# Prompt attention of a streaming encoder: score rows shared between six PSUM banks, and softmax steps and sample copies issued at raised priority

## The chip, the cores and the metric

The kernel runs on one core of one Trainium2 chip. The metric is device time in microseconds (us) of the whole program: three runs of the kernel before gave 2592.65, 2591.31 and 2591.14, the median is 2591.31. Less is better.

A core has several engines, each with a queue of its own: TensorE (PE in the profile; PEld is its weight load) multiplies matrices and transposes, VectorE (DVE) and ScalarE (ACT) do elementwise work, GpSimd (POOL) does some copies and issues some transfers, SyncE (SP) issues most transfers. An engine takes the instructions of its queue in order; a semaphore holds an instruction until its operands are there or its buffer is free. TensorE writes into PSUM, eight banks of 128 partitions by 2 KB; the other engines read them from there.

## The reference

Two groups of frames go through the same two layers with the same weights: a prompt of 512 frames (one stream), and 8 samples of 16 frames each, that continue running streams with 256 cached keys. Cut to what matters:

```python
for l in range(DEPTH):                                   # 2 layers, width 1024
    x = x + 0.5 * swiglu(rmsnorm(x, norm_ffn1[l]), w_ffn1_gu[l], w_ffn1_down[l])   # inner width 2816
    h = rmsnorm(x, norm_mix[l])
    cb, cc, cv, q, k, v, g = split(h @ w_in[l])          # 3 x 512 | 3 x 512 | 2 x 1024
    y_conv = cb * causal_depthwise_conv3(cc * cv)
    s = (q @ k.T) * 64 ** -0.5 + rel_bias                # 8 heads x 64; masked to -1e30:
    y_attn = softmax(where(valid, s, -1e30)) @ v         # own chunk of 64 and the 8 before
    m = sigmoid(g_c) * (y_conv @ w_conv_out) + sigmoid(g_a) * (y_attn @ w_attn_out)
    x = x + m @ w_o
    x = x + 0.5 * swiglu(rmsnorm(x, norm_ffn2[l]), w_ffn2_gu[l], w_ffn2_down[l])
y = rmsnorm(x, norm_final)
```

All data are f32. In the prompt, each frame sees every frame of its own chunk of 64 and all before it (there are only 512), so the scores are a block triangle: row block i (128 queries) has (i + 1) x 128 keys.

## The kernel before

**Staging.** All 640 frames (512 prompt, 128 sample) lie transposed in SBUF, 640 columns wide. Per layer come a feed-forward block, the mixer (projection, convolution, attention, merge) and a second feed-forward block. Weights come from HBM once, in slabs of 128 x 1024 (`load`, L199). To reach f32 accuracy, a slab is split into a rounded part `whi` (ScalarE's cast, L264) and the remainder `wlo` (VectorE, L269), and a product takes three matmuls: whi by xhi, whi by xlo, wlo by xhi. Three slabs of each are kept. `flush` issues remainders that are still pending, `slab` the next slabs' preparation.

**Products in sevens.** A 2 x 2 block product is done in seven block products instead of eight, in the manner of Strassen, over the halves of 320 frames. In the mixer `seven` (L664) does that: products into the PSUM tiles `ma` (the first, third, fifth and last), `mb` (the second) and `mc` (the fourth and sixth). Between them ScalarE and VectorE take intermediate sums out (`c1`, `u2`, `c5`, and the functions `first`, `second`, `third`, `last`). One half of a block product is one step; `seven` is a generator that yields after each, 14 in all. `both` (L908) calls it for q and k, and for the convolution's columns; `gate_pair` (the one at L922) for gates.

**Attention.** `attention` (L1104) computes v, and q and k of the first two heads. Then it goes through four pairs of heads. Its order is written out at the end of the prompt part: `fill(n)` takes n steps of the generator `stream`, which holds the products still to do (q and k of the other pairs, convolution, gates), and so puts them between the parts of the attention:

```python
        fill(2)
        scores(0)
        fill(14)
        for p in range(npair):
            if p + 1 < npair:
                scores(p + 1)
                fill(4)
            vals = values(p)
...
```

- `scores(p)` (L1181): for each of four row blocks, in the order 0, 1, 3, 2, one PSUM tile `pss` per head and one matmul per head (L1200). VectorE then adds the bias and takes the row maximum in one instruction (L1203) and writes the scores into SBUF (`ycp` tiles, named `yc`, for even pairs, `s` tiles for odd pairs). The maxima stand in row 0 of a small tile `st`.
- `weigh` (L1210) calls `softmax` (L1346): VectorE negates the maxima (L1350), ScalarE takes the exponentials and their sums (L1352), VectorE takes the reciprocals (L1354). Then ScalarE scales the four row blocks of a head by them (L1214).
- `values(p)` (L1217): eight groups of transposes of the weights on TensorE (L1227) into tiles `ptp`, copied out by VectorE for the even head and by ScalarE for the odd one, then the products with v into `py`, which ScalarE copies (L1243). Parts of `stream` lie between.
- The samples follow, one after the other: `sscores(b)`, with the same `softmax` inside a raised priority, and `svalues(b)` (L1298). After every fourth sample a bank of transposed results, `ptx`, goes to the tile `yas` (`ya`) by two copies (L1328): VectorE's for the lower 64 partitions, ScalarE's for the upper.

Behind the attention `outputs` (L1018) does the other gate pairs; in each the product tiles are named `qa`, `qb` and `qc`.

**PSUM in the mixer.** `layout("a", 0)` (L158) makes two pools of four banks: `att` for everything of the attention (`pss`, `ptp`, `py` and the samples' tiles), and `pr` for the products (`ma`, `mb`, `mc`). A tile takes the next buffer of its pool in rotation; who writes it first waits until the buffer's previous tile has been read. `seven` asks for its three tiles at its start (L667).

**What sets the order.** In the attention only TensorE's order is the program's (`manual_schedule` for PE, L949). VectorE's, ScalarE's, GpSimd's and SyncE's orders are made when the program is built, by the framework's scheduler: it goes by dependences and by a priority, which is the position in the program. `soon()` (L324) lifts what stands under it by 300 positions, `weights()` in `seven` by 150. So where an instruction stands in VectorE's queue is set by its own position and by whether others were lifted past it. In `outputs` and the feed-forward blocks all of PE, DVE and ACT go in program order.

Of the kernel before, what the change touches and what calls it, by code (L numbers as in the profile page):

```python
# [13 lines left out]
ALU = mybir.AluOpType  # L14
PSUM = bass.MemoryType.PSUM

P = 128
D = 1024
L = 2
SEQ = 512  # L20
NB = 8
TS = 16
T = SEQ + NB * TS
HT = T // 2
PAST = 256
H = 8
HD = 64
# [11 lines left out]
NEG = -1e30  # L39
# [103 lines left out]
def trunk(ctx: ExitStack, tc: tile.TileContext, xin, wst, small, pbias, samplebias, kcache, vcache,  # L143
          yout, ko, vo, co):
    nc = tc.nc
    PE, DVE, ACT, POOL, SP = nc.tensor, nc.vector, nc.scalar, nc.gpsimd, nc.sync
# [24 lines left out]
    def att(name):  # L171
        return banks["att"].tile([P, 512], F32, tag="att", name=name)
# [14 lines left out]
    slabs, n = [], 0  # L187
# [79 lines left out]
    def flush():  # L267
        for lo, src, hi in pending:
            DVE.tensor_tensor(out=lo, in0=src, in1=hi.bitcast(F32), op=ALU.subtract)  # L269
        pending.clear()  # L270
# [16 lines left out]
    def ahead():  # L287

        source(len(ready))

    def begin():

        prep(used[0] + 2)
# [6 lines left out]
    def chunk():  # L300
        return slab()[0]
# [22 lines left out]
    def soon():  # L324
        return tc.high_priority(offset=300)
# [19 lines left out]
    def block(ps, s, half, ops, ks, start, stop):  # L345

        for kp in ks:
            w = [z[:, (half * NP + kp) * P : (half * NP + kp + 1) * P] for z in s]
            xh, xl = ops(kp)
            for j, (a, b) in enumerate(((w[0], xh), (w[0], xl), (w[1], xh))):  # L350
                PE.matmul(ps, a, b, start=start and kp == 0 and j == 0,  # L351
                          stop=stop and kp == NP - 1 and j == 2, skip_group_check=True)
# [16 lines left out]
    for k in range(KT):  # L369
# [4 lines left out]
        if k % 2 == 0:  # L374
            c = slice(k * P, (k + 2) * P)
# [68 lines left out]
    class Expand(Stats):  # L444
# [72 lines left out]
        def weights(self, m):  # L517


            if m == KT - 3:  # L520
                source(used[0] + 3)
            elif m == KT - 1:
                self.flush()
                ahead()
                flush()
                begin()
# [137 lines left out]
    def seven(n, bank, X, c1, u2, c5, first, second, third, last):  # L664


        pa, pb, pc = (bank(f"m{i}{n}")[:, :HT] for i in "abc")  # L667

        def mul(ps, s, half, x, start):
            for ks in (range(NP // 2), range(NP // 2, NP)):  # L670
                block(ps, s, half, x, ks, start, True)
                yield

        def weights():
            with tc.high_priority(offset=150):
                return chunk()

        s = weights()
        yield from mul(pa, s, 0, X["11"], True)
        with soon():  # L680
            ACT.copy(c1, pa)
        yield from mul(pb, s, 1, X["21"], True)
        with soon():
            first(pb)
        s = weights()
        yield from mul(pa, s, 0, X["N6"], False)
        with soon():
            ACT.copy(u2, pa)
        yield from mul(pc, s, 1, X["T5"], True)
        with soon():  # L690
            ACT.copy(c5, pc)
        s = weights()
        yield from mul(pa, s, 0, X["T7"], False)
        with soon():
            second(pa)
        yield from mul(pc, s, 1, X["22"], False)
        with soon():
            third(pc)
        s = weights()
        yield from mul(pa, s, 0, X["T4"], False)  # L700
        with soon():
            last(pa)
# [401 lines left out]
    def attention(l, h, norms, stats, ops, mp, yas, ycp, both, others):  # L1104
# [3 lines left out]
        npair = H // 2  # L1108
        nt = T // P
        NQ = SEQ // P  # L1110
# [5 lines left out]
        qa, ka = {}, {}  # L1116
# [32 lines left out]
        for c in range(KT // 2):  # L1149
            wh, wl = chunk()  # L1150
            for kk in range(2):
# [3 lines left out]
                for t in range(nt):  # L1155
                    for j, (w, xx) in enumerate(((wh, xh), (wh, xl), (wl, xh))):
                        PE.matmul(pv[t], xx[:, t * P : (t + 1) * P],  # L1157
                                  w[:, kk * AW : (kk + 1) * AW],
                                  start=c == 0 and kk == 0 and j == 0,
                                  stop=c == KT // 2 - 1 and kk == 1 and j == 2)  # L1160
# [16 lines left out]
        offs = [sum(P * (i + 1) for i in range(n)) for n in range(NQ)]  # L1177

        weights = {}

        def scores(p):  # L1181

            heads = [2 * p + e for e in range(2)]
            bias, ss, st = [], [], []
            for hh in heads:
                n = f"{l}_{hh}"
                bias.append(mp.tile([P, SEQ], F32, name=f"bias{n}", tag="bias"))
                POOL.dma_start(bias[-1], pbias[l, hh])
                POOL.memset(bias[-1][0:CHUNK, SEQ - CHUNK :], NEG)

                ss.append(mp.tile([P, offs[-1] + SEQ], F32, name=f"s{n}", tag="s") if p % 2
                          else ycp[hh % 2].rearrange("p a t -> p (a t)"))
                st.append(mp.tile([P, 4, NQ], F32, name=f"st{n}", tag="st", bufs=4))

            for i in (0, 1, NQ - 1, *range(2, NQ - 1)):
                w = (i + 1) * P
                pss = [att(f"pss{l}_{hh}_{i}")[:, :w] for hh in heads]
                for e in range(2):
                    r = slice(e * HD, (e + 1) * HD)
                    PE.matmul(pss[e], qa[p][r, i * P : (i + 1) * P], ka[p][r, :w], start=True, stop=True)  # L1200
                for e in range(2):
                    with soon():
                        DVE.tensor_tensor_reduce(  # L1203
                            out=ss[e][:, offs[i] : offs[i] + w], in0=pss[e], in1=bias[e][:, SEQ - w :],
                            scale=1.0, scalar=NEG, op0=ALU.add, op1=ALU.max,
                            accum_out=st[e][:, 0, i : i + 1])
            for e, hh in enumerate(heads):
                weigh(hh, ss[e], st[e])

        def weigh(hh, s, st):  # L1210
            parts = [(offs[i], (i + 1) * P) for i in range(NQ)]
            softmax(s, st, parts)
            for i, (o, w) in enumerate(parts):
                ACT.activation(s[:, o : o + w], s[:, o : o + w], AF.Copy, scale=st[:, 3, i : i + 1])  # L1214
            weights[hh] = s
# [49 lines left out]
        G = 4  # L1265
        held, ptx = {}, [None]
# [31 lines left out]
        def svalues(b):  # L1298
            n = f"{l}_{b}"
            box, st, vraw, vn = held[b]  # L1300
            s = box[:, :KS]
            pt = box[:, KS : KS + 2 * P].rearrange("p (a b) -> p a b", a=2)
            pn, yx = (box[:n, KS + o * P : KS + (o + 1) * P] for n, o in ((TS, 2), (P, 3)))
            ptp = att(f"sptp{n}")
            for j in range(2):
                PE.transpose(ptp[:, j * P : (j + 1) * P], s[:, j * P : (j + 1) * P], ident)
            PE.transpose(ptp[:TS, 2 * P : 3 * P], s[:, PAST:], ident)
            with soon():
                ACT.copy(pt, ptp[:, : 2 * P].rearrange("p (a b) -> p a b", a=2))
                DVE.tensor_copy(pn, ptp[:TS, 2 * P : 3 * P])  # L1310
            yield

            pys = att(f"spy{n}")[:, :P]
            for j, (w, v) in enumerate(((pn, vn), (pt[:, 0], vraw[:, 0]), (pt[:, 1], vraw[:, 1]))):
                for p in range(npair):
                    r = slice(32 * p, 32 * p + 32)
                    PE.matmul(pys[r], w[:, r], v[:, p * P : (p + 1) * P], start=j == 0, stop=j == 2)
            with soon():
                ACT.activation(yx, pys, AF.Copy, scale=st[:, 3, 0:1])
            yield  # L1320
            if b % G == 0:
                ptx[0] = att(f"ptx{n}")
            PE.transpose(ptx[0][:, (b % G) * P : (b % G + 1) * P], yx, ident)
            if b % G == G - 1:
                c0 = SEQ + (b + 1 - G) * TS
                for e in range(2):
                    r = slice(e * HD, (e + 1) * HD)
                    (ACT.copy if e else DVE.tensor_copy)(  # L1328
                        yas[r, :, c0 : c0 + G * TS].rearrange("p a (b t) -> p a b t", b=G),
                        ptx[0][r].rearrange("p (b a e t) -> p a b e t", b=G, a=npair, e=2)[:, :, :, e, :])  # L1330

        sscores(0)
        sscores(1)
        for b in range(NB):
            vals = svalues(b)
            fill(4)
            next(vals)
            fill(3)
            if b + 2 < NB:
                sscores(b + 2)  # L1340
            next(vals)
            fill(2)
            next(vals, None)
        fill(KT * KT)

    def softmax(s, st, parts):  # L1346


        n = len(parts)
        DVE.tensor_scalar(out=st[:, 1, :n], in0=st[:, 0, :n], scalar1=-1.0, scalar2=None, op0=ALU.mult)  # L1350
        for i, (o, w) in enumerate(parts):
            ACT.activation(s[:, o : o + w], s[:, o : o + w], AF.Exp, bias=st[:, 1, i : i + 1],  # L1352
                           accum_out=st[:, 2, i : i + 1])
        DVE.reciprocal(st[:, 3, :n], st[:, 2, :n])  # L1354

    def conv(l, c, pair, upper, c5, rr2, cn, y):

# [278 lines left out]
```

## Time and profile before

The profiled execution is one run of its own, with its own time.

| what | value | where |
|---|---|---|
| median of three runs | 2591.31 us | times |
| time of the profiled execution | 2593.46 us | times |
| its span | 2591.4 us | profile, first line |
| mean granted TensorE clock | 0.997 | cores |
| TensorE at work between 492.15 and 672.53 us (layer 0), 1771.6 and 1951.09 us (layer 1) on the attention and what lies between | 180.4 and 179.5 us | timeline |

How to read it: the page begins with each engine's busy time and its share of the span, then shows the span in forty slices, the transfers, the chain of work that ended last (followed back from the last instruction), and the costliest groups of instructions. A group is named by its line in the code, its engine, its operation and its tiles (`out<-in`, buffer numbers left out). The trace behind the page is asked for other views: waits (which instruction waited, what released it, total, times and longest in us), a timeline (start, duration, engine, line, operation, and in brackets the idle time before it with its releaser), and windows (each engine's busy time in a stretch, with the granted TensorE clock). Duration and idle time of a matmul are modelled: TensorE starts the next before the last has drained, so that a matmul of 320 columns is listed with 0.31 us and the next starts some 0.147 us later.

### The profile page before, as it was taken

What the parts mean: (1) busy time and instruction counts of PE and PEld (TensorE: products, weight loads), DVE (VectorE), ACT (ScalarE), POOL (GpSimd) and SP (SyncE); (2) the same over time, 40 slices, a digit from 0 to 9 for tenths busy, and PEclk for the clock granted to TensorE, in tenths of its full rate; (3) what the DMA queues carried; (4) which work ended last, traced back from release to release, by engine and by line L of the source; (5) the groups of instructions that cost most, each with busy time, mean ns of one, the idle gap of its engine ahead of it and who ended that gap; (6) DMA issues with size and microseconds to landing.
All of it is one profiled execution on the core that took longest, in us unless ns stands there. A gap on an engine that the chain in (4) does not pass through costs nothing.

```text
span 2591.4 us, 42546 instructions
## 1 busy us (share of the span) xinstructions
PE 2563.7 (99%) x17576; PEld 2502.9 (97%) x17576; DVE 1935.0 (75%) x2973; ACT 1147.9 (44%) x1802; POOL 61.4 (2%) x153
## 2 busy tenths in 40 slices
PE   8999999999999999999999999999999999999998
PEld 8999999888999999999999999998899999999998
DVE  7787768677777987767787767786776778877676
ACT  5343335574444543333454333356644445433332
POOL 0000000111000000000000000001110000000000
PEclk9999999999999999999999999999999999999999
DMA  3222223324222232222222222232342222222222
GB/s 132 66 99 92 79 81 101 108 93 161 93 74 90 68 104 82 74 90 82 82 82 98 74 90 82 74 100 97 122 160 78 79 82 82 95 85 74 89 90 74
DMA packets 74066, 237.06 MB, mean 91 GB/s; under 512 B 8240, under 2 KB 19120, under 8 KB 73872
## 3 DMA queue, kind: packets, MB, share of 16 engines
q1 hardware_dynamic: 70272, 223.90, 26.0%
q0 software_dynamic: 2880, 9.79, 1.1%
q8 instruction: 138, 2.26, 0.4%
q10 hardware_dynamic: 720, 0.65, 0.1%
q14 instruction: 56, 0.46, 0.1%
HBM read 225.85 MB, written 7.94 MB: 90 GB/s over the span
## 4 chain that ended last, share of the span: by engine, by line
PE 93%; DVE 4%; ACT 1%; issue 1%; DMA 0%; SPq 0%; DVEq 0%; ACTq 0%
PE pab L351 12%; PE pda L337 11%; PE pdb L337 11%; PE paa L351 11%; PE pcb L351 6%; PE pca L351 5%; PE py L337 4%; PE po L337 4%; PE qa L351 4%; PE pbb L351 3%; PE pba L351 3%; PE ma_cv L351 2%; PE pv L1157 2%; PE ma_qk L351 2%; PE qc L351 2%; PE mc_qk L351 1%
## 5 line engine op out<-in xcount | busy, mean ns | idle before, releaser
L269 DVE TENSOR_TENSOR wlo<-raw,whi 128x1024 fp32r<-128x1024 f32 (+2 forms) x540 | 562.8, 1048 | 193.2 <-ACT whi L264 191.0
L264 ACT CAST whi<-raw 128x1024 fp32r<-128x1024 f32 (+2 forms) x540 | 490.7, 912 | 264.0 <-PE pca L351 79.4
L351 PE MATMUL pab<-xhib,whi 128*128 128x320 f32 x704 | 218.4, 310 | 0.4 <-ACT u_b L788 0.4
L351 PE MATMUL pab<-xlob,whi 128*128 128x320 f32 x704 | 217.5, 309 | 0.0
L351 PE MATMUL pab<-xhib,wlo 128*128 128x320 f32 x704 | 217.5, 309 | 0.0
L351 PE MATMUL paa<-xhia,whi 128*128 128x320 f32 x640 | 198.2, 310 | 0.7 <-ACT c_a L724 0.5
L351 PE MATMUL paa<-xloa,whi 128*128 128x320 f32 x640 | 197.6, 309 | 0.0
L351 PE MATMUL paa<-xhia,wlo 128*128 128x320 f32 x640 | 197.6, 309 | 0.0
L337 PE MATMUL pda<-ahia,whi 128*128 128x320 f32 x704 | 160.6, 309 | 0.6 <-DVE x L854 0.6
L264 ACT CAST whi<-s 128x1024 fp32r<-128x1024 f32 (+1 forms) x120 | 109.5, 913 | 116.3 <-DVE s L208 88.0
L337 PE MATMUL pda<-aloa,whi 128*128 128x320 f32 x704 | 160.4, 309 | 0.0
L337 PE MATMUL pda<-ahia,wlo 128*128 128x320 f32 x704 | 160.4, 309 | 0.0
L337 PE MATMUL pdb<-alob,whi 128*128 128x320 f32 x656 | 149.5, 309 | 0.0
L337 PE MATMUL pdb<-ahib,wlo 128*128 128x320 f32 x656 | 149.4, 309 | 0.0
L337 PE MATMUL pdb<-ahib,whi 128*128 128x320 f32 x656 | 149.4, 309 | 0.0
L269 DVE TENSOR_TENSOR wlo<-s,whi 128x1024 fp32r<-128x1024 f32 (+1 forms) x120 | 126.9, 1058 | 8.6 <-ACT whi L264 8.6
L351 PEld LDWEIGHTS pab<-xhib,whi 128*128 128x128 f32 x704 | 132.2, 188 | 1.2 <-ACT u_b L788 0.9
L351 PEld LDWEIGHTS pab<-xlob,whi 128*128 128x128 f32 x704 | 132.2, 188 | 0.2
L351 PEld LDWEIGHTS pab<-xhib,wlo 128*128 128x128 f32 x704 | 132.2, 188 | 0.0
L351 PEld LDWEIGHTS paa<-xhia,whi 128*128 128x128 f32 x640 | 120.2, 188 | 1.3 <-ACT c_a L724 0.8
L351 PEld LDWEIGHTS paa<-xloa,whi 128*128 128x128 f32 x640 | 120.2, 188 | 0.1
L351 PEld LDWEIGHTS paa<-xhia,wlo 128*128 128x128 f32 x640 | 120.2, 188 | 0.0
(582 smaller groups left out, 6969.1 us busy)
## 6 DMA issues: line engine op xcount, KB each, us to landing
raw<-in_wst SPq DMA_DIRECT2D x384, 512.0 KB, 3.5
kc<-in_kcache SPq DMA_DIRECT2D x32, 256.0 KB, 3.9
vc<-in_vcache SPq DMA_DIRECT2D x16, 512.0 KB, 4.3
bias<-in_pbias POOLq DMA_DIRECT2D x16, 256.0 KB, 3.1
x<-in_xin SPq DMA_DIRECT2D x8, 320.0 KB, 6.5
out_vo<-v POOLq DMA_DIRECT2D x10, 256.0 KB, 2.5
out_ko<-k POOLq DMA_DIRECT2D x8, 320.0 KB, 2.4
out_yout<-x SPq DMA_DIRECT2D x8, 192.0 KB, 1.9
```

The costliest lines, as they stand in the source:

```text
L264: ACT.copy(hi[:, d], src[:, c])
L269: DVE.tensor_tensor(out=lo, in0=src, in1=hi.bitcast(F32), op=ALU.subtract)
L337: PE.matmul(ps[:, a, :HT], w, x[:, a * HT : (a + 1) * HT], start=k == 0 and j == 0, stop=k == n - 1 and j == 2)
L351: PE.matmul(ps, a, b, start=start and kp == 0 and j == 0, stop=stop and kp == NP - 1 and j == 2, skip_group_check=True)
L1157: PE.matmul(pv[t], xx[:, t * P : (t + 1) * P], w[:, kk * AW : (kk + 1) * AW], start=c == 0 and kk == 0 and j == 0, stop=c == KT // 2 - 1 a ...
```

## The change

Four things are edited, all in the mixer.

1. `scores`: the eight row blocks of a pair of heads (four each) go into six tiles instead of eight. Row blocks 0 and 2 of a head share one tile of 128 + 384 columns, row blocks 3 and 1 have one each. The two tiles of row block 1 (one per head) come from the pool `pr` instead of `att`. Order of the matmuls: rows 0, 2, 3, 1. A tile's reads are issued behind all its matmuls.
2. `seven`: the tiles `ma`, `mb` and `mc` are asked for just ahead of their first matmul, and no longer all at the start. Since `scores` now takes two tiles from `pr` between steps of `seven`, the order of asking sets which buffer each gets.
3. `softmax`: the negated maxima (L1350) and the reciprocals (L1354) stand under `soon()`.
4. `svalues`: the two copies of a `ptx` bank (L1328) stand under `soon()`.

```diff
@@ -664,7 +664,8 @@
     def seven(n, bank, X, c1, u2, c5, first, second, third, last):
 
 
-        pa, pb, pc = (bank(f"m{i}{n}")[:, :HT] for i in "abc")
+        def new(i):
+            return bank(f"m{i}{n}")[:, :HT]
 
         def mul(ps, s, half, x, start):
             for ks in (range(NP // 2), range(NP // 2, NP)):
@@ -675,10 +676,11 @@
             with tc.high_priority(offset=150):
                 return chunk()
 
-        s = weights()
+        s, pa = weights(), new("a")
         yield from mul(pa, s, 0, X["11"], True)
         with soon():
             ACT.copy(c1, pa)
+        pb = new("b")
         yield from mul(pb, s, 1, X["21"], True)
         with soon():
             first(pb)
@@ -686,6 +688,7 @@
         yield from mul(pa, s, 0, X["N6"], False)
         with soon():
             ACT.copy(u2, pa)
+        pc = new("c")
         yield from mul(pc, s, 1, X["T5"], True)
         with soon():
             ACT.copy(c5, pc)
@@ -1192,18 +1195,25 @@
                           else ycp[hh % 2].rearrange("p a t -> p (a t)"))
                 st.append(mp.tile([P, 4, NQ], F32, name=f"st{n}", tag="st", bufs=4))
 
-            for i in (0, 1, NQ - 1, *range(2, NQ - 1)):
-                w = (i + 1) * P
-                pss = [att(f"pss{l}_{hh}_{i}")[:, :w] for hh in heads]
-                for e in range(2):
-                    r = slice(e * HD, (e + 1) * HD)
-                    PE.matmul(pss[e], qa[p][r, i * P : (i + 1) * P], ka[p][r, :w], start=True, stop=True)
-                for e in range(2):
-                    with soon():
-                        DVE.tensor_tensor_reduce(
-                            out=ss[e][:, offs[i] : offs[i] + w], in0=pss[e], in1=bias[e][:, SEQ - w :],
-                            scale=1.0, scalar=NEG, op0=ALU.add, op1=ALU.max,
-                            accum_out=st[e][:, 0, i : i + 1])
+            for rows in ((0, 2), (3,), (1,)):
+                pss = [(pr if rows == (1,) else att)(f"pss{l}_{hh}_{rows[0]}") for hh in heads]
+                spans, o = [], 0
+                for i in rows:
+                    spans.append((i, slice(o, o + (i + 1) * P)))
+                    o = spans[-1][1].stop
+                for i, c in spans:
+                    for e in range(2):
+                        r = slice(e * HD, (e + 1) * HD)
+                        PE.matmul(pss[e][:, c], qa[p][r, i * P : (i + 1) * P], ka[p][r, : (i + 1) * P],
+                                  start=True, stop=True)
+                for i, c in spans:
+                    for e in range(2):
+                        w = (i + 1) * P
+                        with soon():
+                            DVE.tensor_tensor_reduce(
+                                out=ss[e][:, offs[i] : offs[i] + w], in0=pss[e][:, c],
+                                in1=bias[e][:, SEQ - w :], scale=1.0, scalar=NEG, op0=ALU.add,
+                                op1=ALU.max, accum_out=st[e][:, 0, i : i + 1])
             for e, hh in enumerate(heads):
                 weigh(hh, ss[e], st[e])
 
@@ -1325,9 +1335,10 @@
                 c0 = SEQ + (b + 1 - G) * TS
                 for e in range(2):
                     r = slice(e * HD, (e + 1) * HD)
-                    (ACT.copy if e else DVE.tensor_copy)(
-                        yas[r, :, c0 : c0 + G * TS].rearrange("p a (b t) -> p a b t", b=G),
-                        ptx[0][r].rearrange("p (b a e t) -> p a b e t", b=G, a=npair, e=2)[:, :, :, e, :])
+                    with soon():
+                        (ACT.copy if e else DVE.tensor_copy)(
+                            yas[r, :, c0 : c0 + G * TS].rearrange("p a (b t) -> p a b t", b=G),
+                            ptx[0][r].rearrange("p (b a e t) -> p a b e t", b=G, a=npair, e=2)[:, :, :, e, :])
 
         sscores(0)
         sscores(1)
@@ -1347,11 +1358,13 @@
 
 
         n = len(parts)
-        DVE.tensor_scalar(out=st[:, 1, :n], in0=st[:, 0, :n], scalar1=-1.0, scalar2=None, op0=ALU.mult)
+        with soon():
+            DVE.tensor_scalar(out=st[:, 1, :n], in0=st[:, 0, :n], scalar1=-1.0, scalar2=None, op0=ALU.mult)
         for i, (o, w) in enumerate(parts):
             ACT.activation(s[:, o : o + w], s[:, o : o + w], AF.Exp, bias=st[:, 1, i : i + 1],
                            accum_out=st[:, 2, i : i + 1])
-        DVE.reciprocal(st[:, 3, :n], st[:, 2, :n])
+        with soon():
+            DVE.reciprocal(st[:, 3, :n], st[:, 2, :n])
 
     def conv(l, c, pair, upper, c5, rr2, cn, y):
 
```

In the built program every engine holds the same instructions before and after, differently ordered. TensorE's order differs only in the rows of the score matmuls. On VectorE the negated maxima stand right behind the reads of the scores, and the reciprocals of heads 0 and 1 ahead of the second pair's score reads; on ScalarE the scalings of heads 0 and 1 stand ahead of the second pair's exponentials. In the sample part only the last `ptx` copies move: VectorE's ahead of the second half of a weight remainder, ScalarE's ahead of the second sigmoid of the last pair of gates. Two transfers that SyncE issues change places; GpSimd's order is the same.

## The prediction

> **What bounds the kernel now.** First the page. TensorE is busy nearly all the time, and the chain that ended last lies on it.
>
> ```profile
> span 2591.4 us, 42546 instructions
> PE 2563.7 (99%) x17576; PEld 2502.9 (97%) x17576; DVE 1935.0 (75%) x2973; ACT 1147.9 (44%) x1802; POOL 61.4 (2%) x153
> ...
> PE 93%; DVE 4%; ACT 1%; issue 1%; DMA 0%; SPq 0%; DVEq 0%; ACTq 0%
> ```
>
> The change adds and removes no instruction on any engine, so it can only win where TensorE waits, or where its clock is low. Second view: the waits, TensorE's alone (total us, times, longest).
>
> ```profile
> PE ptp L1227 <- ACT yc L1214: 5.1, 12, 1.3
> PE pss L1200 <- DVE st L1203: 2.2, 3, 0.9
> PE qb L351 <- ACT ya L1328: 1.5, 2, 0.8
> ```
>
> These three, 8.8 us, are all that the diff addresses: transposes that wait for scaled weights, score matmuls that wait for a bank to be read, and the first gate product behind the attention, which waits for the last sample copy. Third view: the stretches from one head pair's scores to the next. Columns: stretch, length, then busy us of PE, PEld, DVE, ACT, POOL, then the granted clock.
>
> ```profile
> 507.57:533.42 25.85, 23.15 (x137) 18.79 (x136) 17.54 (x45) 19.86 (x47) 4.55 (x10) 0.93 0.21 74
> 533.42:553.88 20.46, 20.05 (x137) 17.21 (x136) 14.70 (x38) 13.21 (x34) 3.54 (x10) 1.00 0.36 120
> ...
> 1787.10:1813.14 26.04, 23.36 (x137) 18.98 (x136) 17.52 (x45) 19.84 (x47) 4.54 (x10) 0.93 0.20 74
> 1813.14:1833.26 20.12, 20.04 (x137) 17.21 (x136) 14.55 (x38) 13.24 (x34) 3.51 (x10) 1.00 0.39 122
> ```
>
> With the same 137 matmuls, the first stretch of each layer takes 5 to 6 us more than the second. So the cost is over twice the 2.6 us per layer that the waits view shows. The timeline of the first stretch says why (start, length, engine, line; idle time and releaser in brackets):
>
> ```profile
> 504.84 0.19 ACT L1352 ACTIVATION_READ_ACCUMULATOR yc<-yc,st 128x1 f32 x1
> ...
> 514.83 0.23 DVE L1354 RECIPROCAL st<-st 128x4 f32<-128x4 f32 x2
> ...
> 515.04 0.40 ACT L1214 ACTIVATE yc<-yc,st 128x128 f32<-128x128 f32 x1 [1.98 <-DVE st L1354]
> ...
> 515.58 0.30 PE L1227 MATMUL ptp<-ident,yc 128*128 128x128 f32 x1 [1.34 <-ACT yc L1214]
> 515.65 3.43 ACT L1214 ACTIVATE yc<-yc,st 128x256 f32<-128x256 f32 x7
> ```
>
> The exponentials of heads 0 and 1 end at 505.0; their reciprocals run at 514.8, because they stand in VectorE's queue behind the next pair's scores. Only then does ScalarE scale, and the transposes follow its eight scalings one by one. The same windows view, cut finer, gives the rest:
>
> ```profile
> 514.10:517.00 2.90, 1.06 (x5) 0.42 (x3) 1.09 (x6) 1.96 (x5) 0.29 (x2) 1.00 0.80 271
> 517.00:520.50 3.50, 2.69 (x12) 1.92 (x12) 0.90 (x2) 3.32 (x9) 0.00 (x0) 0.75 0.54 205
> 520.50:523.10 2.60, 2.60 (x14) 2.60 (x13) 0.35 (x1) 2.02 (x7) 0.00 (x0) 0.67 0.00 0
> ```
>
> The granted clock falls to 0.75 and 0.67 behind the broken stretch, and the product there runs slow although it waits for nothing: 2.59 us from its first matmul (520.54) to the next transposes (523.13), against 1.84 (541.75 to 543.59) in the second stretch.
>
> **The change, part by part.**
>
> *Reciprocals and maxima ahead (L1350, L1354).* In the changed order, head 0's reciprocal stands on VectorE right behind the weight remainder of 502.17, and head 1's ahead of the next scores. Head 0's four scalings (some 1.8 us, from eight in 3.7) stand on ScalarE before 506, where it idled 0.88 us before 505.91 and 1.04 before 507.57; head 1's stand ahead of the next pair's exponentials, where it idled 2.79 before 511.30. The last should end near 511.6, and TensorE asks at 514. So the wait goes, and with it the slow clock. Worth: first stretch against second, each without its score waits. Layer 0: (25.85 - 0.05) - (20.46 - 0.41) = 5.8. Layer 1: (26.04 - 0.05) - (20.12 - 0.08) = 5.95. Together **-11.7**.
>
> What the new waits hold up: head 0's reciprocal waits for an exponential ended at 502.8, and its place on VectorE comes at 503.3. Head 1's waits for one that head 0's scalings push back from 504.9 to about 507.4; its place comes at 507.6. Were it late, the remainder of the weights behind it on VectorE would be late too, but TensorE needs that only after the scores and one product, 4.6 us on.
>
> What is late next: in the shortened stretch ScalarE has 19.9 us of work less 1.8 moved out, in 20.1 us. It can take up the pair's exponentials only when the scores are read, 5.5 us after they begin. From there I add its queue in the new order by the rows (eight exponentials 4.4, four scalings of head 2 and four of head 3 3.7, copies out of PSUM 2.1, three weight casts 2.0, the rest) and reach 18.3 us at the cast that VectorE's remainder needs just ahead of the last keys. Remainder and keys take 1.0 more, 19.4; TensorE wants the keys at 19.8. The copies of the first transposes end at 9.5 and 9.9, and TensorE asks for these banks at 9.7 and 10.05. So there is cover, of 0.2 to 0.4 us. New waits: from nothing to 3 us a layer; I take 0.5, nearest to the sums: **+1.0** in all.
>
> *Rows (0,2), (3), (1) in six banks.* Every head pair's eight score matmuls can issue at once. The waits go: 2.2 by the view, and gaps of 0.05 to 0.08 in the other five pairs: **-2.5**. Added: VectorE's first read of a head waits for both rows of its bank. That is 0.6 us later at most (384 of 1280 columns of a block of 2.1 to 2.9 us), below nothing by no reason; hidden, because the first transposes come 6 us after the scores. The raised bank pressure shows at product c: its bank is a lent one, and it waits until row 1 of the first head is read, now next to last. Reads take 0.22, 0.35, 0.48 and 0.61 us by width (start to start), a remainder 0.6 or 1.14; from a start 1.0 to 1.5 after the first score matmul (the latest seen: 553.88 to 555.37) the read ends at 5.1 to 5.2. TensorE reaches c at 6.5 (492.15 to 498.68) in the first pair, at 8.3 (533.42 to 541.75) in the others, since transposes lie between. Cost: nothing, with 1.3 us of cover. Each us beyond costs a us, eight times.
>
> VectorE takes its turn at a bank after TensorE here, never beside it. [...]
>
> *Bank per product only when first written (`seven`).* It issues nothing; it turns the rotation, as counted above.
>
> *Sample copies (L1328).* ScalarE's half of the last copy now stands ahead of the second sigmoid (1.55 us for two), so it ends 0.77 earlier; VectorE's half passes a 0.6 us remainder that is needed 3 us later. TensorE's wait of 0.77 per layer goes: **-1.5**. The sigmoid is 0.4 later; its gate is used tens of us on.
>
> Sum: -11.7 - 2.5 - 1.5 + 1.0 = **-14.7 us**. The profiled run took 2593.46 us (span 2591.4, 2.1 around it), 2.15 above the median of 2591.31. So a run like it should take 2578.8, and the median 2576.6. About 5.2 us (0.2%) is what a measurement can tell from no change.
>
> **The rivals.**
>
> *ScalarE takes the stall's place.* Its cover is 0.2 to 0.4 us at four places. If it is 2.5 us late, TensorE waits some 2.2 a layer at the copies or at the next scores, and the clock falls again (0.75 in the slow product above): 3 us x 2 = 6 instead of 1. Gain 9.7: 2581.6. For it: 18.1 of 20.1 us busy. Against it: the second stretch runs the same queue order with no such wait.
>
> *Only the idle time comes back, not the slow clock.* Then 5.1 + 2.5 + 1.5 - 1 = 8.1: 2583.2. For it: the clock could fall for a reason of its own. Against: 1.00 in all other pairs. [...] Here no gap is over 1.34 us and it fell all the same, in both layers; the trace decides.
>
> *The change doesn't do what it says*: the scaling still comes late, since ScalarE's queue before the second scores is fuller than I count. Then -2.5 - 1.5 remain: 2587.3, inside 0.2%.
>
> *Slower: the lent bank.* If VectorE is behind by more than 1.3 us in the first pair, 3.1 in the others, product c stands still in every pair. At 3 us of wait in each of eight pairs, 24, plus slow clock of 2.2 (the transposes at half pace 1.45, the product 0.75) each, 17.6: 41.6 - 14.7 gives 2618. It outweighs the gain from about 1.8 us of wait per pair. For it: VectorE was 1.5 us late at one block. Against: the cover counted above.
>
> **How the numbers follow.** Forecast as summed (gain 12 to 17): 0.64. ScalarE's place: 0.16. Idle time only: 0.05. Not what it says: 0.08. Lent bank: 0.05. More than 17 (a 0.6 us wait of the sample stage that goes too): 0.02. The likeliest gives 2576.6. The range 2574 to 2584 takes in the first three, with new waits from nothing to 3 us a layer. Faster: 0.64 + 0.16 + 0.05 + 0.02, less 0.02 for the weaker ends, 0.85. Same 0.09, slower 0.06.
>
> **What would show it.** In the waits view the lines of ptp behind ACT and of pss behind DVE are gone, and qb is below 0.2. The first stretch of each layer takes 20 to 21 us at clock 1.00. A new line of ptp behind ACT or DVE copies, or of pss behind the keys, is ScalarE's rival; one of mc behind the score reads is the lent bank. The forecast is wrong if a stretch stays at 23 us or more, or if a gap of over 1 us stands before c.

## The result, and the profile after

The kernel after took 2574.41 us (median of four runs, 2574.16 to 2574.82), the kernel before 2591.22 in the runs beside them: 16.8 us less, a ratio of 0.9934 with a 95% interval of 0.9921 to 0.9946. The forecast was 2576.6. The profiled execution after took 2574.47 us, so it stands for the median. That of before did not: its start-up, up to the first matmul into the tile `npsa`, lasted 27.8 us, that of after and of the ten experiments 25.8 to 26.5; and one wait in the sample part (first layer), which costs 0.75 us, is in no other profile at that size. These 2.0 us are no part of the change. They are why the spans differ by 18.7 and the medians by 16.8.

First the page of after, the same two lines and the chain. TensorE's busy time fell by 10, although its 17,576 instructions are the same. (The first line counts 12 instructions fewer than before; they are semaphore instructions, which the engines' counts below it leave out.)

```profile
span 2572.7 us, 42534 instructions
PE 2553.6 (99%) x17576; PEld 2497.1 (97%) x17576; DVE 1934.1 (75%) x2973; ACT 1144.7 (44%) x1802; POOL 60.5 (2%) x153
...
PE 92%; DVE 4%; ACT 3%; issue 1%; DMA 0%; ACTq 0%; DVEq 0%
```

Then TensorE's waits (total us, times, longest). The three lines of before are gone; two small ones have come, both behind ScalarE's copies out of PSUM: the second group of transposes, and the fifth block product of the first gate pair behind the attention, which waits until ScalarE has copied the third out of the same bank (called the fifth gate product from here on).

```profile
PE ptp L1237 <- ACT pt L1240: 0.9, 4, 0.3
PE qa L351 <- ACT capsm L1047: 0.7, 2, 0.4
```

The four stretches between the scores of one pair and of the next (length, then busy us of PE, PEld, DVE, ACT, POOL, then the granted clock): the first of each layer, 25.85 and 26.04 before, is now the shorter one, and its clock is 1.00.

```profile
505.57:525.16 19.59, 19.59 (x137) 16.84 (x137) 16.54 (x43) 17.60 (x43) 3.23 (x9) 1.00 0.29 98
525.16:545.33 20.17, 19.89 (x137) 16.81 (x136) 15.19 (x40) 14.64 (x39) 3.69 (x10) 1.00 0.39 122
1775.79:1795.37 19.58, 19.58 (x137) 16.84 (x137) 16.52 (x43) 17.58 (x43) 3.22 (x9) 1.00 0.28 98
1795.37:1815.51 20.14, 19.91 (x137) 16.83 (x137) 15.17 (x40) 14.63 (x39) 3.69 (x10) 1.00 0.39 122
```

The timeline of after shows the order that the forecast counted on: the second reciprocal (505.46 to 505.63) stands ahead of VectorE's reads of the next scores, the first of which starts at 506.83, and the last scaling ends at 509.39, 2.2 us ahead of the transposes at 511.55.

```profile
505.46 0.17 DVE L1367 RECIPROCAL st<-st 128x4 f32<-128x4 f32 x1
...
506.52 0.80 ACT L1224 ACTIVATE yc<-yc,st 128x128 f32<-128x128 f32 x2
...
508.68 0.71 ACT L1224 ACTIVATE yc<-yc,st 128x512 f32<-128x512 f32 x1
...
511.55 1.69 PE L1237 MATMUL ptp<-ident,yc 128*128 128x128 f32 x14
```

Laying the two traces of TensorE over each other, block by block (a block's length is the time from its first matmul to the first of the next), gives what each part of the sum measured:

| term | forecast | measured, both layers |
|---|---|---|
| broken stretch (softmax) | -11.7 | -5.75 and -5.94 = -11.7 |
| score blocks (rows) | -2.5 | eight blocks of 2.89 to 3.76 us became 2.36 each: -6.4 |
| wait behind the last sample copy | -1.5 | -1.05 and -1.04 = -2.1 |
| new waits | +1.0 | second transposes of the second and third pair 0.46, 0.51, 0.43, 0.54, and a product behind them 0.15 twice: +2.2; fifth gate product 0.66 and 0.64: +1.3 |
| sum | -14.7 | -16.6, added before rounding |

### The profile page after: what moved, and what is told of

Its sections match the earlier page's. It is cut to its first block, busy times and chain, and to the rows that moved or that the text cites. A ratio compares the mean times of both kernels' runs of the same rounds, so it can differ in the third digit from the quotient of the medians.

```text
span 2572.7 us, 42534 instructions
## 1 busy us (share of the span) xinstructions
PE 2553.6 (99%) x17576; PEld 2497.1 (97%) x17576; DVE 1934.1 (75%) x2973; ACT 1144.7 (44%) x1802; POOL 60.5 (2%) x153
## 3 DMA queue, kind: packets, MB, share of 16 engines
q8 instruction: 138, 2.26, 0.4%
## 4 chain that ended last, share of the span: by engine, by line
PE 92%; DVE 4%; ACT 3%; issue 1%; DMA 0%; ACTq 0%; DVEq 0%
PE pab L351 12%; PE pda L337 12%; PE pdb L337 11%; PE paa L351 11%; PE pcb L351 6%; PE pca L351 5%; PE py L337 4%; PE po L337 4%; PE qa L351 4%; PE pbb L351 3%; PE pba L351 3%; PE pv L1160 2%; PE ma_cv L351 2%; PE ma_qk L351 2%; PE qc L351 2%; PE ma_b L351 1%
```

## The experiments

Each ran beside runs of the kernel before; gains are against these (medians 2591.75 to 2592.06). The theory after the result: the forecast's mechanisms are right, but a wait for a bank costs far more than the view of waits lists. Its rival: the score waits were worth 2.5, and the surplus came with the softmax edit.

**Softmax edit alone.** To the kernel before:

```diff
-        DVE.tensor_scalar(out=st[:, 1, :n], in0=st[:, 0, :n], scalar1=-1.0, scalar2=None, op0=ALU.mult)
+        with soon():
+            DVE.tensor_scalar(out=st[:, 1, :n], in0=st[:, 0, :n], scalar1=-1.0, scalar2=None, op0=ALU.mult)
...
-        DVE.reciprocal(st[:, 3, :n], st[:, 2, :n])
+        with soon():
+            DVE.reciprocal(st[:, 3, :n], st[:, 2, :n])
```

> The kernel before with the third edit alone (reciprocals and negated maxima raised). Theory: the four edits add up, and this one is worth the broken stretch alone, 11.7 us: about 2579.5, with the first stretch of each layer at clock 1.00 and the score blocks still 2.9 to 3.7 us long. Rival (only the idle time returns, the clock falls for a reason of its own): 5 us, 2586. Second rival (the surplus of the measured 16.8 over the forecast 14.7 comes with this edit): 2577 or less.

2579.8 us, a gain of 12.3 (ratio 0.9951, 0.9937 to 0.9965). The broken stretch gives 5.75 and 5.94 in the trace, and the clock stands at 1.00, as the windows of this kernel show:

```profile
505.71:525.81 20.10, 20.05 (x137) 17.22 (x136) 16.24 (x43) 17.77 (x43) 3.11 (x9) 1.00 0.25 95
...
1779.05:1799.16 20.11, 20.06 (x138) 17.23 (x137) 16.25 (x43) 17.77 (x43) 3.12 (x9) 1.00 0.26 96
```

"Only the idle time comes back" (5.1 listed) falls. The wait behind the last sample copy went too (2.1), though the copies were not touched. Against these 13.8 stand a score block in each layer that became 0.6 and 0.9 us longer (3.82) and the new wait of the fifth gate product, 0.52 a layer. That leaves 11.3 in the trace, a little under the 12.3 of the medians.

**Reciprocals alone.** The same without the first half of the diff.

> The kernel before with the reciprocals alone raised (one of the two raised instructions of the third edit). Theory: the reciprocals were what stood behind the second pair's score reads, so this alone ends the broken stretch: 2579.8, as with both. Rival: raising the negated maxima carries part of it, by letting the second pair's exponentials start earlier: 2581 or more, with a wait of the first transposes left.

2580.18 us, a gain of 11.7 (0.9953, 0.9941 to 0.9966); the broken stretch gives 5.75 and 5.94, as with both. So the reciprocals carry the gain, and raising the maxima beside them brings nothing that shows.

**Rows and banks alone.** The first two edits (`scores` and `seven`) on the kernel before.

> The kernel before with the first and second edit alone (score rows in six banks, tiles of the products asked for late). Theory: the score blocks shrink from 2.9 to 3.7 us to 2.36 us, eight times, 6.4 us together, of which about 1.9 comes back as waits of the second transposes for ScalarE's copies: 2585 to 2587. Rival (the forecast's term, only the listed waits return): 2.5 us, 2588.7. The broken stretch stays 25 us with a clock of about 0.93.

2588.78 us, a gain of 3.3 (0.9987, 0.9978 to 0.9995): by the time, the rival's number. By the trace it is the theory's: all eight blocks are 2.36 us long, 6.4 saved; but 3 come back behind ScalarE, which is no earlier than before. (The profiled execution, 2587.18, is the shortest of the eleven, 1.6 below their median, so these sums stand for it alone.) These waits of the kernel's trace say it: the transposes wait 5.6 for scalings where they waited 5.1, and 1.5 more for copies.

```profile
PE ptp L1237 <- ACT yc L1224: 5.6, 10, 1.8
...
PE ptp L1237 <- ACT pt L1240: 1.5, 3, 0.6
```

**Sample copies alone.** The fourth edit on the kernel before.

> The kernel before with the fourth edit alone (last sample copies raised). Theory: the first gate product behind the attention starts 1.0 us earlier per layer, but the copy of its first tile stands behind the delayed sigmoid, and the next product on that tile waits 0.5: net 0.5 per layer, 2590.2. Rival (the forecast's term): 0.77 per layer, 2589.7, with no new wait. The times are too close; the line of the gate product behind the copy of the first tile tells them apart.

2591.18 us, a gain of 0.9 (0.9996, 0.9987 to 1.0005), not to be told from nothing. In the trace the product comes 0.72 earlier in each layer, of the 1.04 that the wait had cost, and the fifth gate product gives 0.33 back: 0.4 net, nearer to the theory. The line by which the two were to be told apart is not in the view of waits; the lengths alone show it. The three parts alone sum to 16.5 us, together they gave 16.8. That they meet is partly chance: the wait behind the last sample copy is counted in the first part and in the third.

**The change without the sample copies.** The fourth edit undone in the kernel after.

> The kernel after without the fourth edit (sample copies not raised). Theory: with the third edit in, the bank of the last sample results no longer comes to the first gate product's second tile, so that nothing waits for the copy, and the fourth edit adds nothing: 2574.4, with no wait of that product. Rival (the forecast's term): each edit is worth its own wait, 0.5 to 0.8 per layer: 2575.4 to 2576.

2573.73 us, a gain of 18.1 (0.9929, 0.9917 to 0.9942); the interval overlaps that of after. Between the start-up and the last matmul the two traces drift 0.3 us apart, nearly all of it at the fifth gate product, which is 0.14 and 0.13 earlier without the fourth edit. So the fourth edit adds nothing to the others. In the built program the product behind the attention has no wait for ScalarE's copy at all: with the softmax edit in, the rotation gives it another bank.

**No lent banks.** In the kernel after:

```diff
-                pss = [(pr if rows == (1,) else att)(f"pss{l}_{hh}_{rows[0]}") for hh in heads]
+                pss = [att(f"pss{l}_{hh}_{rows[0]}") for hh in heads]
```

> The kernel after, but row block 1's two tiles come from the attention's own four banks, so that they wait until rows 0 and 2 of the same head are read. Theory: a bank wait tears the two heads' matmuls apart, which run side by side, and costs more than the idle time that the view of waits lists: first head about 0.3 us late, second 0.9, so some 0.9 us per block, eight times 7 us: 2581 (2579 to 2584), with listed idle time of only about 2 us. Rival (a wait costs its listed idle time): 2576.4.

2585.5 us (0.9975, 0.9966 to 0.9985): 11 lost of the 17. The score blocks take 3.41 us, one 3.76, instead of 2.36: 8.8 us in sum. And the view of waits lists half a microsecond of it:

```profile
PE qa L351 <- ACT ya L1339: 3.6, 2, 1.8
...
PE pss L1207 <- DVE st L1213: 0.5, 1, 0.5
```

Its timeline shows the first block (eight matmuls, listed as 16 instructions) as one unbroken run of 3.49 us, where the kernel after has 2.43; the kernel before, whose view of waits lists 2.2 us for all eight blocks, has 2.98 there, unbroken too. In this order, without lending, after, before:

```profile
490.55 3.49 PE L1207 MATMUL pss<-k,q 64*128 64x128 f32 x16
```

```profile
490.65 2.43 PE L1207 MATMUL pss<-k,q 64*128 64x128 f32 x16
```

```profile
492.15 2.98 PE L1200 MATMUL pss<-k,q 64*128 64x128 f32 x16
```

The theory stands and was too small: a record of these matmuls (64 rows) is listed with 0.27 to 0.69 us in the kernel before, and the matmuls of the two heads of a pair start 7 ns apart, side by side, when nothing holds them. In that kernel's first block the matmuls of row block 3 wait for their banks, and there the two heads start 0.23 us apart, listed with 0.69 us each: the first head's listed duration covers the second's wait. So that wait shows as length, and as idle time the trace has 0.05 us, ahead of the first head. The other line costs 2.1 us a layer more: in this rotation the first gate product gets the bank of the last sample results. In the second layer the clock also falls behind this wait of 1.8 us, and the two products there take 1.6 us longer. The window with the wait, and the next:

```profile
1936.98:1940.39 3.41, 1.60 (x12) 1.32 (x11) 2.96 (x6) 3.33 (x5) 0.00 (x0) 1.00 0.00 0
1940.39:1943.80 3.41, 3.41 (x14) 3.41 (x14) 0.00 (x0) 1.06 (x3) 0.00 (x0) 0.50 0.00 0
```

Against this the new waits of the kernel after, 3.5 us, are gone. So 8.8 + 4.1 + 1.6 - 3.5 gives the 11.

**Half of the stall back.** In the kernel after, head 1's reciprocal is left at its own place:

```diff
-            softmax(s, st, parts)
+            softmax(s, st, parts, hh != 1)
...
-        with soon():
+        with soon() if early else nullcontext():
             DVE.reciprocal(st[:, 3, :n], st[:, 2, :n])
```

> The kernel after, with the reciprocal of head 1 of each layer not raised (head 0's still is): half of the first pair's scalings come late again. Theory: the stall's price is idle time plus a low clock behind it, so that even half of the late scalings brings most of it back: some 2.2 us of one gap and four paced transposes, then the clock below 0.9, 4 to 6 us a layer: 2583 to 2586. Rival (the clock does not fall behind one gap with fewer paced transposes): idle time alone, 2.5 to 3 us a layer: 2579.5 to 2580.5.

2584.07 us (0.9969, 0.9956 to 0.9981): 9.7 above the kernel after. The transposes take 3.7 us longer in both layers, with idle gaps of 2.26, 0.17 and 0.28 in the first and 2.27, 0.18 and 0.28 in the second. But the clock fell in the second layer only. Windows of this kernel, the transposes and the product behind them, layer 0 and then layer 1:

```profile
511.28:516.39 5.11, 2.32 (x16) 1.51 (x14) 2.42 (x8) 5.11 (x15) 0.56 (x3) 1.00 0.83 280
516.39:518.24 1.85, 1.85 (x15) 1.84 (x14) 0.52 (x1) 1.85 (x4) 0.00 (x0) 1.00 0.19 78
1785.09:1790.27 5.18, 2.38 (x16) 1.57 (x14) 2.50 (x8) 5.18 (x15) 0.58 (x3) 0.99 0.85 293
1790.27:1793.60 3.33, 3.33 (x15) 3.31 (x13) 0.45 (x1) 1.92 (x5) 0.00 (x0) 0.50 0.05 20
```

The same product, 1.85 us at a clock of 1.00 and 3.33 at 0.50. The median lies in the theory's range, but in this execution neither theory held for both layers: one paid 3.7 us, the other 5.2. With nearly the same stall in both, the layers differ in where it lies on the grid of the clock's falls (last section); that this is the reason is not shown. The other four runs took 1.2 to 1.8 us longer than the profiled one; that would fit a fall in both layers, but no trace of them shows it.

**Three attempts at what is late next**, all on the kernel after. The first: negated maxima in two instructions.

```diff
-        with soon():
-            DVE.tensor_scalar(out=st[:, 1, :n], in0=st[:, 0, :n], scalar1=-1.0, scalar2=None, op0=ALU.mult)
+        for a in range(min(n, 2)):
+            with soon():
+                DVE.tensor_scalar(out=st[:, 1, a:n:2], in0=st[:, 0, a:n:2], scalar1=-1.0, scalar2=None, op0=ALU.mult)
```

> The kernel after, with the negated maxima of a head computed in two instructions, rows 0 and 2, then rows 1 and 3, instead of one for all four (two instructions more per pair of heads). Theory: what is late after the change is ScalarE, which stands idle 4.6 us until the last row of a pair is read before it can begin its exponentials; begun some 2 us earlier, it copies the second pair's transposes in time, and four waits of about 0.47 us go: 2572.5. Rival: the exponentials start earlier but the copies' place in the queue stays: 2574.4. Second rival: the added instructions delay VectorE's reads, and the lent bank, with 0.2 us of cover in the first pair, is read too late: up to 1 us slower.

2577.86 us (0.9945, 0.9931 to 0.9959): 3 slower in the trace. All three expectations missed. The exponentials start earlier (the first of the first pair at 494.12, against 496.91 in the kernel after), but scalings and casts made ready earlier stand ahead of ScalarE's copies out of PSUM: in the first pair product c now waits for the copy of its own bank, and the transposes wait 0.2 to 0.5 more. Lines from the waits and from ScalarE's timeline:

```profile
PE mc_qk L351 <- ACT c L694: 1.0, 2, 0.5
```

```profile
498.01 1.31 ACT L1224 ACTIVATE yc<-yc,st 128x128 f32<-128x128 f32 x3
499.23 1.03 ACT L264 CAST whi<-raw 128x1024 fp32r<-128x1024 f32 x1
500.17 0.41 ACT L694 COPY c<-mc_qk 128x320 f32<-128x320 f32 x1
```

The second: reciprocals raised in the first pair only (`early` is `hh < 2` in the diff of the half stall).

> The kernel after, with the reciprocals raised for the first pair of heads of a layer alone. Theory: the 0.45 to 0.54 us by which the second transposes of the second and third pair wait for ScalarE's copy are the price of shorter score blocks (the row edit), so nothing changes: 2574.4, the four waits still there. Rival: they are the price of scalings that raised reciprocals put ahead of the copies: 1.9 us less, 2572.5.

2575.94 us (0.9939, 0.9926 to 0.9951), 2.1 later at the end of the trace. Neither: the four waits double instead of staying or going.

```profile
PE ptp L1237 <- ACT pt L1240: 2.6, 4, 0.6
```

So raised reciprocals help the later pairs too, about 0.4 us each. The third: the odd head's first transposed tile copied by VectorE.

```diff
-                    (ACT.copy if e else DVE.tensor_copy)(pt[e][:, at[j] : at[j] + w], ptp)
+                    (ACT.copy if e and j else DVE.tensor_copy)(pt[e][:, at[j] : at[j] + w], ptp)
```

> The kernel after, with the odd head's first transposed tile copied by VectorE instead of ScalarE. Theory: in the second and third pair the second group of transposes waits because this copy stands on ScalarE behind two scalings; VectorE is idle then, so at least half of the four waits of 0.45 to 0.54 us goes: 2572.5 to 2573.5. Rival: the odd head's second tile, still ScalarE's and now behind three scalings, is late instead: 2574.4 or more. Second rival: VectorE's other copies come 0.6 later and hold the transposes: 2576.

2575.58 us (0.9936, 0.9922 to 0.995); the first rival: the second tile is late in its place, and the wait behind ScalarE stays.

```profile
PE ptp L1237 <- ACT pt L1240: 1.2, 3, 0.4
```

None of the ten programs is shown to beat the kernel after; only the one without the sample copies is level with it.

## Why the prediction was right

- **Reciprocals ahead** was sized right, 11.7 against 11.7. Comparing a stretch with its neighbour, instead of adding up listed waits (5.1), was the step that did it; the slow product (2.59 us against 1.84) came from a clock of 0.50 that went with the stall: with the softmax edit alone the clock of that stretch is 1.00.
- **Rows in six banks** was the term mis-sized: 2.5 forecast, 6.4 measured. The step that failed is "2.2 by the view, and gaps of 0.05 to 0.08 in the other five pairs": it took the listed idle time for the price of a wait. The length of the blocks was in the trace, 2.89 to 3.76 us for the same eight matmuls; the run without lent banks shows how such waits hide.
- **Cover of the lent bank** was mis-sized too: 1.3 us forecast in the first pair, 0.5 measured. Product c waits for the read of the first head's row block 1, which ends at 496.09, 0.3 later within its block than counted; and product c starts at 496.63, 0.55 earlier within it than before, because the block shrank by that much. In the other pairs 2.5 to 2.8 are left, where 3.1 were counted. Nothing waited, so the rival with the lent bank did not come, but its distance was less than told.
- **What is late next** was named rightly, ScalarE's copies, but with 1.0 instead of 2.2, and at the wrong place. The forecast had counted its thin cover in the shortened first stretch; there nothing waits. The waits stand in the second and third pair, though the forecast had held up the second stretch as one that runs "with no such wait": the score blocks ahead of them shrank most (0.6 to 1.4 us, against 0.5), so TensorE comes to the copies earlier. That the rows alone bring waits there and the softmax edit alone does not bears this out. The waits of the transposes take back a third of what the rows give. The sign of ScalarE's rival, a line of `ptp` behind ScalarE's copies, did come, but with 0.9 listed, far from the 6 of that rival. The first attempt speaks against ScalarE's idle time as the cause: used for earlier work, it made the copies later. That what stands ahead of a copy in its queue decides fits all three attempts, but is not shown alone, and why raised reciprocals ease the later pairs was not settled.
- **Sample copies** was right about the wait and wrong about its owner: the softmax edit turns the rotation, and the wait goes without the fourth edit. And "its gate is used tens of us on" overlooked the queue: behind the sigmoid stands, after six casts, the copy for which the fifth gate product waits. TensorE now comes earlier and waits 0.52 for it without the fourth edit, and 0.65 with it, since the sigmoid is later.
- The forecast came out 2.2 us high, and the traces explain 2.0 of it: 3.9 too little for the rows stood against 1.2 too little for the new waits of the transposes and 0.7 too much for the copies. That these errors cancelled by half is luck.

VectorE's turn at a bank stayed as the prediction has it: in the profiled executions before and after, every read of the scores starts behind the end of the last matmul into its bank, by 0.04 us at the least before and 0.13 after. With two rows in a bank this cost no time: VectorE's first read, 0.65 later in the first pair's block than before (1.28 against 0.63), is hidden as counted. And the clock fell behind short gaps: ahead of its falls in the attention no gap is over 1.34 us in the kernel before, and none over 2.27 with half of the stall.

## What to carry to other kernels

Size a wait by the length of a stretch against the same work elsewhere, not by listed idle time: without lent banks the score blocks were 8.8 us longer and 0.5 of it was listed, because the durations of overlapping matmuls hid their waits. An instruction of 0.2 us that stood behind the wrong queue cost 5.75 and 5.94 us a layer here: the engine behind it stalled, TensorE waited, and the work behind then ran for 3.41 us at a clock of 0.50. When one edit changes the order in which banks come free, ask again which other waits it has already removed.

## What the runs showed of the hardware

In the mixer the slow clock read 0.50 and lasted 3.41 us (in the run with the copies alone once 6.8, two such stretches in a row), and its falls sit on a grid: the falls in the two layers lie 1280.00 us apart in the kernel before, 1280.00 with the copies alone and 1276.59 with the rows alone. These distances differ by 3.41, the length of one such stretch, and are 375, 375 and 374 steps of 3.4133 us (1280.00 over 375). Windows of the kernel before, the step ahead of the fall and the fall itself:

```profile
515.38:518.79 3.41, 2.17 (x7) 0.97 (x7) 0.69 (x1) 3.41 (x9) 0.29 (x2) 1.00 0.84 292
518.79:522.20 3.41, 3.13 (x14) 3.06 (x14) 0.56 (x1) 3.04 (x10) 0.00 (x0) 0.50 0.09 35
```

TensorE was not idle ahead of the fall: seven records, 2.17 us of listed work. In the run with half of the stall, the step ahead of the fall (layer 1) held nine records; in layer 0, where the same grid, carried back by 1280.00 us, cuts the same stall in two, the steps held 13 and 14, and no clock was lost:

```profile
510.18:513.59 3.41, 1.70 (x13) 1.45 (x11) 3.39 (x12) 2.93 (x10) 1.21 (x3) 1.00 0.51 163
513.59:517.00 3.41, 2.33 (x14) 1.76 (x15) 0.65 (x2) 3.41 (x9) 0.14 (x1) 1.00 0.82 288
```

```profile
1786.77:1790.18 3.41, 1.69 (x9) 1.13 (x10) 0.73 (x3) 3.41 (x10) 0.29 (x2) 1.00 0.92 332
1790.18:1793.43 3.25, 3.25 (x15) 3.25 (x14) 0.54 (x1) 2.00 (x4) 0.00 (x0) 0.50 0.07 26
```

So much the same stall had two prices here, 3.7 and 5.2 us. What sets off a fall stays open. It is not the number of records: the step ahead of the fall without lent banks held 12, and so did a step of the run with the rows alone that no fall followed (first line below). In the steps shown, the weight loads (PEld) put them in order: 0.97 to 1.32 us ahead of a fall, 1.36 and more where none came. But near the end of the kernel before, other work with 1.70 us of weight loads stands ahead of a fall at 2583.84 (second line), after which the clock reads 0.50 to the end of the span, 7.5 us.

```profile
509.35:512.76 3.41, 1.61 (x12) 1.36 (x11) 3.04 (x11) 0.94 (x3) 1.07 (x2) 1.00 0.39 144
```

```profile
2580.43:2583.84 3.41, 1.87 (x16) 1.70 (x14) 3.34 (x8) 1.07 (x3) 0.00 (x0) 1.00 0.51 181
```
